# A hybrid decoder trunk on one core: rows of the activations' buffer of 2560 instead of 2112 bytes, low half 1536 instead of 1088 bytes behind the high one, and a dynamic DMA scratch of 8 instead of 16 KB

## Chip, core and metric

The kernel runs on one core of a Trainium2 chip. The metric is the time of one execution in microseconds, as the device measures it; the time of a kernel is the median of its runs. A profile of one execution shows what each engine did: TensorE (PE for matmuls, PEld for the loading of their weights), VectorE (DVE), ScalarE (ACT), GpSimd (POOL), SyncE (SP, which issues DMAs here) and the DMA queues.

## The reference

A sequence of 256 positions of width 1024 passes six sublayers: feed-forward, forgetting attention, feed-forward, then feed-forward, HGRN2 (a gated linear recurrence), feed-forward. Each has an RMS norm with a shift and a scale ahead of it and a gate behind it, which come from a conditioning vector `c`; all in float32. Cut to its core:

```
mod = (silu(c) @ ada_w[i] + ada_b[i]).reshape(B, 3, 3, 1, D)
h = rms_norm(x, norm_g[i, 0]) * (1 + mod[:, 0, 1]) + mod[:, 0, 0]
a, b = split(h @ w_up); x = x + 0.5 * mod[:, 0, 2] * ((silu(a) * b) @ w_down)
h = ...; x = x + mod[:, 1, 2] * (fox_attention(h, ...) or hgrn2(h, ...))
h = ...; x = x + 0.5 * mod[:, 2, 2] * swiglu(h, ...)
return rms_norm(x, final_norm_g)
```

The feed-forward is 1024 to 2 x 2816 and back; the two mixers have four projections of 1024 x 1024 and one back.

## The kernel before

**Split products.** To get float32 results from `float32r` matmuls, every operand is kept as a high and a low half, each 32 bits wide: the high half is the value rounded, the low half what is left. `mm3` (L724 to L731) makes one product of a 128 x 128 piece of weights with the activations of one row: weights' high half times activations' high half (L728), weights' high half times activations' low half (L729), weights' low half times activations' high half (L730), all added into one PSUM tile. Each of the three is 256 columns wide and has its own weight load.

**Where the activations lie.** Two buffers `hbuf[0]` and `hbuf[1]` hold the activations of a sublayer, one for the normed input `h`, the other for the next one (`ubuf`) or for the output of a mixer; `out_proj` swaps them. Each has 8 rows (one for each 128 of the 1024 features; a "row" here is what one partition holds for it). A row has the 256 positions of the high half, then two columns with the norm's shift (`HS`), which the "folded" blocks read along, so that their matmuls of L728 and L730 are 258 columns wide, then a gap, and from column `LO` on the 256 of the low half. `LO` and the row's length `HB` are set at the head of the file:

```
HS = S + 2
LO = S + 16
HB = LO + S
```

The lines that write a low half are L589, L655, L704 and L795, those that read it L729 and L880 (`hl` of L877). The inner activations of the feed-forward lie in another tile, `gx` (in `big`): 22 rows of 512 columns, the low half directly behind the high one, so 1024 bytes behind, with a row every 2048 bytes. Products on `hbuf` write PSUM tiles named `pf`, those on `gx` tiles named `pd`; both go through `mm3`.

**Weights.** SP fetches weights in raw pieces of up to 512 KB into 8 buffers (`raw`), in a fixed order of items (`plan`). ACT copies a piece to `wh` (L369, rounding), DVE subtracts to get `wl` (L370). There are three `wh` and three `wl` buffers of 8 KB per partition; a block of the up projection is 1024 x 256 weights and 48 matmuls. Between the weights stand pieces of the matrices for the conditioning, 512 KB each, which DVE multiplies and adds (L408, L410); their sums pass through PE in `ada_finish` as short matmuls (L469). The order of everything is set by `tick`, which `mm3` calls after each three matmuls: it splits the next piece when it is due and steps the side tasks.

**The start.** The first feed-forward's first 7 blocks run row by row while their weights and the conditioning's matrices arrive (`head_products`, 112 calls of `mm3`).

**Addresses.** All tiles lie one behind the other in each partition, in the order of their making: 16384 bytes of dynamic DMA scratch, four constants of 32 bytes, `big` (45056), `ident` (512), `hbuf[0]`, `hbuf[1]`, the rest. `big`, and with it `gx`, begins at 128 modulo 512; so do `hbuf[0]` (at 62080) and `hbuf[1]` (78976). `wh` and `wl` begin at 448 modulo 512, and each of their rows of 256 columns is 1024 bytes. A row of `hbuf` is 2112 bytes, 4 x 512 + 64, and its low half stands 1088 = 2 x 512 + 64 bytes behind.

| | high half, modulo 512 | low half, modulo 512 |
|---|---|---|
| `gx`, any row | 128 | 128 |
| `hbuf`, row k, before | 128 + 64 k | 192 + 64 k |
| `hbuf`, row k, changed | 128 | 128 |

**Scratch.** It serves the DMAs that POOL issues. There are four: two of a bias (L600), `tm` (L603) and `lmask` (L604).

Of the kernel before, what the change touches and what calls it, by code (L numbers as in the profile page):

```python
# [19 lines left out]
P = 128  # L20
S = 256
# [32 lines left out]
ADA_HEAD = 5  # L54
ADA_TAIL = 6
HS = S + 2
LO = S + 16
HB = LO + S


def shape_constants():
    i = np.arange(P)
    ident = np.eye(P, dtype=np.float32)
    causal = np.where(i[None, :] > i[:, None], np.float32(NEG), np.float32(0)).astype(np.float32)
    lcross = (i[:, None] > i[None, :]).astype(np.float32)
    masks = np.zeros((P, len(LEV), P), np.int32)
    for li, b in enumerate(LEV):
        masks[:, li] = i[:, None] // b == i[None, :] // b
    sel32 = (i[:, None] % 32 == np.arange(32)[None, :]).astype(np.float32)
    selq = np.zeros((P, 16), np.float32)  # L70
    for h in range(16):
        selq[h, h] = -1
        selq[64 + h, h] = -1
    consts = np.concatenate([ident, causal, selq, sel32], axis=1)
    return (np.ascontiguousarray(consts), np.ascontiguousarray(lcross),
            np.ascontiguousarray(masks.reshape(P, -1)))


def flip(x):
    return np.ascontiguousarray(np.concatenate([x[:, :P], x[:, :P - 1:-1]], axis=1))  # L80
# [10 lines left out]
class Trunk:  # L91
# [404 lines left out]
    def setup(self):  # L496
# [82 lines left out]
        for q in range(D // QW):  # L579
# [3 lines left out]
            for k in range(q * n, (q + 1) * n):  # L583
# [4 lines left out]
                v0 = nc.scalar.copy(h[:, :S], u)  # L588
                v1 = nc.vector.tensor_tensor(h[:, LO:LO + S], u, h[:, :S].bitcast(F32), ALU.subtract)  # L589
                self.last_shift = (v0.ins, v1.ins)  # L590
# [58 lines left out]
    def x_ready(self, k):  # L649
        nc = self.nc  # L650
        if self.fold:
            gs = self.mod(*self.fold, "gs")[:, k:k + 1]
            u = self.ubuf[:, k, :]
            nc.scalar.activation(u[:, :S], self.x[:, k, :], AF.Copy, scale=gs)
            nc.vector.scalar_tensor_tensor(u[:, LO:LO + S], self.x[:, k, :], gs, u[:, :S].bitcast(F32),  # L655
                                           ALU.mult, ALU.subtract)
# [43 lines left out]
    def h_shift(self, u, k, l, s, dst):  # L700
        nc = self.nc
        sh = self.mod(l, s, "shift")
        a = nc.scalar.activation(dst[:, k, :S], u, AF.Identity, bias=sh[:, k:k + 1])
        v = nc.vector.scalar_tensor_tensor(dst[:, k, LO:LO + S], u, sh[:, k:k + 1], dst[:, k, :S].bitcast(F32),  # L704
                                           ALU.add, ALU.subtract)
# [162 lines left out]
    def v_token(self, kind, h, dst, func):  # L868
        nc = self.nc
        pss = [self.acc("pv0"), self.acc("pv1")]  # L870
        for kh in range(2):
            wh, wl = self.weights(kind)
            for i in range(4):
                k = kh * 4 + i
                for t in range(2):
                    hh = self.h[:, k, t * P:(t + 1) * P]
                    hl = self.h[:, k, LO + t * P:LO + (t + 1) * P]  # L877
                    nc.tensor.matmul(pss[t], hh, wh[:, i, :], start=(k == 0), stop=False)  # L878
# [392 lines left out]


def build(inputs, subs=(0, 1, 2, 3, 4, 5), final=True):
    nc = bacc.Bacc("TRN2", target_bir_lowering=False, num_devices=1)
    arrays, args = {}, {}
    consts, tmat, lmask = shape_constants()
    every = {n: np.ascontiguousarray(inputs[n]) for n in _INS}
    every["x"] = flip(every["x"])
    every.update(consts=consts, tmat=tmat, lmask=lmask)
    for name, arr in every.items():  # L1280
        arrays[f"in_{name}_dram"] = arr
        args[name] = nc.dram_tensor(f"in_{name}_dram", arr.shape, mybir.dt.from_np(arr.dtype),
                                    kind="ExternalInput").ap()
    out = nc.dram_tensor("out_0_dram", (1, S, D), F32, kind="ExternalOutput").ap()
    with tile.TileContext(nc) as tc:
        with ExitStack() as ctx:
            Trunk(ctx, tc, args, out, list(subs), final).run()
    return nc, arrays
# [6 lines left out]
```

## Time and profile before

| | us |
|---|---|
| median of 3 runs | 1092.43 |
| the three runs | 1087.57, 1092.43, 1092.46 |
| the profiled execution | 1088.01 |
| its span, first to last instruction | 1086.2 |

The mean granted TensorE clock of the profiled execution was 0.994. Its stages, from the rows that write the tiles: the start to about 65 us; the first feed-forward to 216; attention to 365; the second feed-forward to 553; the third to 741; HGRN2 to 888; the last feed-forward and the output to the end. Matmuls are pipelined: the duration that a row of the trace shows for one is longer than the distance to the next one's start.

### The profile page before, as it was taken

The page shows a single profiled execution, that of the slowest core. Times are in us where ns is not written, and L with a number is a line of the kernel's source. Part 1 is how long each engine was busy: PE and PEld are TensorE (multiplying, and loading weights), DVE is VectorE, ACT ScalarE, POOL GpSimd, SP SyncE. Part 2 cuts the span into 40 slices and gives each one's busy share as a digit, 9 for nine tenths or more (in the row PEclk, how much of TensorE's full clock was granted, in tenths as well). Part 3 has the DMA queues.
Part 4 walks back from the last instruction along what each step waited for, and adds up shares of the span by engine and source line. Part 5 has one row for each costly group of instructions (what it writes and reads, how often), then busy time and mean ns, then how long its engine had stood idle before and what let it go on. Part 6 is the DMA issues. An engine that isn't in the chain of part 4 may idle for free.

```text
span 1086.2 us, 22135 instructions
## 1 busy us (share of the span) xinstructions
PE 1058.2 (97%) x8835; PEld 1036.9 (95%) x8835; DVE 882.5 (81%) x1593; ACT 587.0 (54%) x1100; POOL 23.1 (2%) x46
## 2 busy tenths in 40 slices
PE   5999999999999999999999999999999999999997
PEld 5999999988999999999999999999998999999996
DVE  6999999589995999898779999978977879555542
ACT  5464444476864755443555444446677756444443
POOL 0000000020000000000000000000000000000000
PEclk8999999999999999999999999999999999999998
DMA  9999999669784589999959999985633366665531
GB/s 292 337 330 327 330 349 315 176 209 341 251 263 122 156 252 324 331 302 305 263 170 274 335 331 355 318 243 177 211 117 117 118 169 188 187 194 179 179 109 40
DMA packets 304707, 260.26 MB, mean 240 GB/s; under 512 B 9524, under 2 KB 281500, under 8 KB 304604
## 3 DMA queue, kind: packets, MB, share of 16 engines
q1 hardware_dynamic: 304172, 257.80, 77.9%
q8 instruction: 69, 1.13, 0.4%
q0 software_dynamic: 288, 0.52, 0.2%
q10 hardware_dynamic: 144, 0.52, 0.1%
q14 instruction: 34, 0.28, 0.1%
HBM read 257.77 MB, written 1.05 MB: 238 GB/s over the span
## 4 chain that ended last, share of the span: by engine, by line
PE 73%; issue 18%; ACT 3%; DVE 3%; DMA 1%; POOL 1%; SPq 0%; POOLq 0%; DVEq 0%
PE pf L730 16%; PE pf L728 16%; PE pf L729 16%; PE pd L728 6%; PE pd L730 6%; PE pd L729 6%; PE pv L878 1%; PE pv L879 1%; PE pv L880 1%; ACT wh L369 1%; PE sc L999 1%; DVE wl L370 1%; PE pA L1173 1%; DMA raw<-in_ffn_w_up_dram 1%; PE pt L1021 1%
## 5 line engine op out<-in xcount | busy, mean ns | idle before, releaser
L730 PE MATMUL pf<-hbuf,wl 128*128 128x256 f32 (+1 forms) x1920 | 541.7, 283 | 0.0
L729 PE MATMUL pf<-hbuf,wh 128*128 128x256 f32 x1920 | 536.5, 280 | 0.9 <-DVE hbuf L589 0.9
L728 PE MATMUL pf<-hbuf,wh 128*128 128x256 f32 (+1 forms) x1920 | 535.8, 283 | 0.6 <-ACT hbuf L588 0.6
L369 ACT CAST wh<-raw 128x1024 fp32r<-128x1024 f32 x338 | 341.4, 1028 | 284.2 <-PE pf L729 165.4
L370 DVE TENSOR_TENSOR wl<-raw,wh 128x1024 fp32r<-128x1024 f32 x338 | 401.0, 1195 | 107.1 <-ACT wh L369 106.1
L729 PEld LDWEIGHTS pf<-hbuf,wh 128*128 128x128 f32 x1920 | 363.2, 189 | 1.4 <-DVE hbuf L589 1.1
L730 PEld LDWEIGHTS pf<-hbuf,wl 128*128 128x128 f32 x1920 | 361.8, 188 | 0.2 <-issue 0.2
L728 PEld LDWEIGHTS pf<-hbuf,wh 128*128 128x128 f32 x1920 | 359.7, 189 | 1.3 <-ACT hbuf L588 0.7
L728 PE MATMUL pd<-gx,wh 128*128 128x256 f32 x704 | 195.6, 278 | 0.0
L729 PE MATMUL pd<-gx,wh 128*128 128x256 f32 x704 | 194.7, 277 | 0.0
L730 PE MATMUL pd<-gx,wl 128*128 128x256 f32 x704 | 194.7, 277 | 0.0
L410 DVE SCALAR_TENSOR_TENSOR adaacc<-raw,cond,adaacc 128x1024 f32<-128x1024 f32 x112 | 143.7, 1283 | 12.9 <-DMA raw<-in_ada_w_dram 11.7
L728 PEld LDWEIGHTS pd<-gx,wh 128*128 128x128 f32 x704 | 132.4, 188 | 0.1
L729 PEld LDWEIGHTS pd<-gx,wh 128*128 128x128 f32 x704 | 132.2, 188 | 0.0
L730 PEld LDWEIGHTS pd<-gx,wl 128*128 128x128 f32 x704 | 132.2, 188 | 0.0
L793 ACT CAST gx<-g 128x256 fp32r<-128x256 f32 x88 | 35.6, 406 | 66.7 <-DVE g L835 58.2
L795 DVE TENSOR_TENSOR gx<-g,gx 128x256 fp32r<-128x256 f32 x88 | 36.9, 421 | 0.5 <-ACT gx L793 0.2
L835 DVE TENSOR_TENSOR g<-sa,pf 128x256 f32<-128x256 f32 x73 | 30.0, 414 | 0.1
L800 DVE SCALAR_TENSOR_TENSOR x<-pd,mod,x 128x256 f32<-128x256 f32 x32 | 14.3, 479 | 19.0 <-PE pd L730 19.0
L462 DVE STREAM_TRANSPOSE adatr<-adaacc 128x256 f32<-128x256 f32 x64 | 28.4, 443 | 1.5
L463 DVE TENSOR_REDUCE adared<-adatr 128x8 f32<-128x256 f32 x64 | 26.7, 417 | 1.4
L834 ACT ACTIVATE sa<-pf 128x256 f32<-128x256 f32 x73 | 27.4, 376 | 0.0
(219 smaller groups left out, 871.2 us busy)
## 6 DMA issues: line engine op xcount, KB each, us to landing
raw<-in_ffn_w_up_dram SPq DMA_DIRECT2D x162, 512.0 KB, 6.1
raw<-in_ada_w_dram SPq DMA_DIRECT2D x128, 512.0 KB, 6.2
raw<-in_ffn_w_down_dram SPq DMA_DIRECT2D x76, 512.0 KB, 5.5
raw<-in_fox_w_in_dram SPq DMA_DIRECT2D x32, 512.0 KB, 5.2
raw<-in_hgrn_w_in_dram SPq DMA_DIRECT2D x32, 512.0 KB, 4.5
raw<-in_ada_w_dram SPq DMA_DIRECT2D x32, 256.0 KB, 6.7
raw<-in_ffn_w_up_dram SPq DMA_DIRECT2D x16, 448.0 KB, 5.9
raw<-in_fox_w_out_dram SPq DMA_DIRECT2D x8, 512.0 KB, 4.5
```

The source lines that it names most:

```text
L369: nc.scalar.copy(wh[:, ks, cs], raw)
L370: nc.vector.tensor_tensor(wl[:, ks, cs], raw, wh[:, ks, cs].bitcast(F32), ALU.subtract)
L410: nc.vector.scalar_tensor_tensor(self.ada_acc, raw, self.cond[:, k:k + 1], self.ada_acc, ALU.mult, ALU.add)
L462: nc.vector.transpose(tr, total[:, o:o + S])
L463: nc.vector.tensor_reduce(red[:, o // 32:(o + S) // 32], tr.rearrange("p (b j) -> p b j", j=32), AX.X, ALU.add)
L728: nc.tensor.matmul(ps, wh, hx[:, :n], start=first, stop=False, skip_group_check=True)
L729: nc.tensor.matmul(ps[:, :S], wh, hx[:, lo:lo + S], start=False, stop=False, skip_group_check=True)
L730: nc.tensor.matmul(ps, wl, hx[:, :n], start=False, stop=last, skip_group_check=True)
L793: nc.scalar.copy(dst[:, :S], v)
L795: nc.vector.tensor_tensor(dst[:, lo:lo + S], v, dst[:, :S].bitcast(F32), ALU.subtract)
L834: nc.scalar.activation(sa, ps[0], AF.Silu)
L835: nc.vector.tensor_tensor(g, sa, ps[1], ALU.mult)
```

## The change

Two numbers. `LO` is 384 columns instead of 272, so a row of `hbuf` (`HB`) is 640 columns, 2560 bytes, and the low half stands 1536 bytes behind the high one. The unused gap between the shift's columns and the low half grows from 14 to 126 columns. Both buffers grow by 3584 bytes, and the dynamic DMA scratch shrinks from 16384 to 8192 bytes.

```diff
-LO = S + 16
+LO = S + P
 HB = LO + S
...
 def build(inputs, subs=(0, 1, 2, 3, 4, 5), final=True):
-    nc = bacc.Bacc("TRN2", target_bir_lowering=False, num_devices=1)
+    nc = bacc.Bacc("TRN2", target_bir_lowering=False, num_devices=1, dynamic_dma_scratch_size=8192)
```

The instructions of each engine and their order stay as they are; only addresses differ. `big`, `ident` and `hbuf[0]` move down by 8192 bytes, `hbuf[1]` by 4608, all behind it by 1024; every tile begins at the same offset modulo 512 as before.

## Prediction

> **What bounds the kernel now.** I read the page first: busy shares, then the chain that ended last.
>
> ```profile
> span 1086.2 us, 22135 instructions
> ...
> PE 1058.2 (97%) x8835; PEld 1036.9 (95%) x8835; DVE 882.5 (81%) x1593; ACT 587.0 (54%) x1100; POOL 23.1 (2%) x46
> ...
> PE 73%; issue 18%; ACT 3%; DVE 3%; DMA 1%; POOL 1%; SPq 0%; POOLq 0%; DVEq 0%
> PE pf L730 16%; PE pf L728 16%; PE pf L729 16%; PE pd L728 6%; PE pd L730 6%; PE pd L729 6%; PE pv L878 1%; PE pv L879 1%; PE pv L880 1%; ACT wh L369 1%; PE sc L999 1%; DVE wl L370 1%; PE pA L1173 1%; DMA raw<-in_ffn_w_up_dram 1%; PE pt L1021 1%
> ```
>
> TensorE sets the end. The chain lies on the three matmuls of `mm3` (L728 to L730), and 48% of the span on those that write `pf`, which read `hbuf`. The waits say the same: first those of PE, then those of ACT.
>
> ```profile
> PE adac L446 <- DVE adc L434: 3.4, 1, 3.4
> PE pv L546 <- DMA ident<-in_consts_dram: 3.1, 1, 3.1
> ...
> ACT wh L369 <- PE pf L729: 165.4, 70, 7.2
> ...
> ACT wh L358 <- DMA raw<-in_ffn_w_up_dram: 19.8, 9, 3.2
> ```
>
> PE's longest waits are 3.4 and 3.1 us and lie in the start; no weight tile is among them. ACT, which begins each split of a weight, waits 165.4 us for PE to release an old `wh`. So weights stand ready, and what PE needs per matmul is what counts. L358 is the start (the first 65 us), where ACT waits for DMA: nothing is gained there.
>
> **The rate, row by row.** The mean of one matmul (280 ns) is a modelled, pipelined duration; the rate is the distance between starts. First the number of matmuls, from the groups by form:
>
> ```profile
> L729 PE MATMUL pf<-hbuf,wh 128*128 128x256 f32 x1920 | 536.5, 280 | 0.9 <-DVE hbuf L589 0.9
> L730 PE MATMUL pf<-hbuf,wl 128*128 128x256 f32 x1584 | 446.0, 283 | 0.0
> ...
> L730 PE MATMUL pf<-hbuf,wl 128*128 128x258 f32 x336 | 95.7, 285 | 0.0
> ...
> L728 PE MATMUL pd<-gx,wh 128*128 128x256 f32 x704 | 195.6, 278 | 0.0
> ```
>
> So 3 x 1584 = 4752 plain matmuls on `hbuf`, 3 x 336 = 1008 of the folded blocks (two of three with 258 columns), and 3 x 704 = 2112 on `gx`. Now the timeline of PE: first and last row of stretches that hold nothing but `mm3`. On `gx` (187 rows, 186 distances):
>
> ```profile
> 496.79 0.28 PE L729 MATMUL pd<-gx,wh 128*128 128x256 f32 x1
> ...
> 517.87 0.28 PE L729 MATMUL pd<-gx,wh 128*128 128x256 f32 x1
> ```
>
> 21.08 us / 186 = 113.3 ns. On `hbuf`, two stretches (113 rows, then 114 rows):
>
> ```profile
> 465.80 0.28 PE L730 MATMUL pf<-hbuf,wl 128*128 128x256 f32 x1
> ...
> 478.87 0.28 PE L728 MATMUL pf<-hbuf,wh 128*128 128x256 f32 x1
> ...
> 939.77 0.28 PE L729 MATMUL pf<-hbuf,wh 128*128 128x256 f32 x1
> ...
> 953.09 0.28 PE L728 MATMUL pf<-hbuf,wh 128*128 128x256 f32 x1
> ```
>
> 13.07 us / 112 = 116.7 ns and 13.32 us / 113 = 117.9 ns: the same instructions, weights and column count as on `gx`, 3.4 to 4.6 ns slower. They keep one of these two rates until something else passes through PE. Within a stretch the distances depend on the row of `hbuf`:
>
> ```profile
> 943.07 0.29 PE L730 MATMUL pf<-hbuf,wl 128*128 128x256 f32 x1
> 943.20 0.28 PE L728 MATMUL pf<-hbuf,wh 128*128 128x256 f32 x1
> 943.32 0.27 PE L729 MATMUL pf<-hbuf,wh 128*128 128x256 f32 x1
> 943.43 0.28 PE L730 MATMUL pf<-hbuf,wl 128*128 128x256 f32 x1
> ```
>
> Going from row 5 to row 6 they are 0.13, 0.12 and 0.11 us. On `hbuf`, the rows' phase modulo 512 moves by 64 bytes from row to row and the low half stands 64 bytes behind the high one; on `gx` every row and both halves have the same phase, 128. That is what the change gives to `hbuf`. The weights keep their phase (448) in both. The folded blocks (90 rows) and a later stretch on `gx` (88 rows):
>
> ```profile
> 384.75 0.28 PE L728 MATMUL pf<-hbuf,wh 128*128 128x258 f32 x1
> ...
> 395.49 0.28 PE L730 MATMUL pf<-hbuf,wl 128*128 128x258 f32 x1
> ...
> 1049.75 0.28 PE L730 MATMUL pd<-gx,wl 128*128 128x256 f32 x1
> ...
> 1060.00 0.28 PE L730 MATMUL pd<-gx,wl 128*128 128x256 f32 x1
> ```
>
> 10.74 us / 89 = 120.7 ns folded; 10.25 us / 87 = 117.8 ns on `gx`, after four transposes of the output (`fin`) had passed. So equal phases too know a **short state** (113.3) and a **long one** (117.8), and keep either until disturbed.
>
> **The change part by part.** No instruction is added, removed or moved; only addresses differ.
>
> *Plain matmuls.* Of the 4752, 3 x 112 = 336 belong to the start, which waits for DMA. Left: 4416. Their present rate I take as 117.4 ns (a third of the blocks at 116.7, the rest at 117.9; the last feed-forward's row in the table below has 682 in 80 us, two of them across its edges, so 117.6). All in the short state they gain 4.1 ns each, 18.1 us; all in the long one they lose 0.4 ns each, 1.8 us. I take four fifths short: 0.8 x 18.1 - 0.2 x 1.8 = 14.1 us. It is nearer to the short end since on `gx` the long state appears only behind the output's transposes.
>
> *Folded blocks.* Bounds: nothing gained, or 113.3 ns stretched by two columns in two of three (113.9): 6.8 ns x 1008 = 6.9 us. I take their surcharge over the long state (120.7 - 117.8 = 2.9) as kept: 116.2 ns, so 4.5 us, and four fifths of it, 3.6. Sum so far 17.7 us.
>
> *What lies beside.* The same gain has to be fed. Stretches of the span in a table, with DMA share and GB/s last:
>
> ```profile
> 395.00:475.00 80.00, 80.00 (x692) 79.69 (x691) 74.16 (x102) 37.20 (x56) 0.00 (x0) 1.00 1.09 322
> 475.00:525.00 50.00, 50.00 (x448) 49.70 (x447) 46.14 (x64) 22.14 (x32) 0.00 (x0) 1.00 0.89 293
> 600.00:680.00 80.00, 79.99 (x697) 79.46 (x696) 78.00 (x107) 37.07 (x56) 0.00 (x0) 1.00 1.11 340
> ...
> 220.00:365.00 145.00, 141.91 (x1099) 131.30 (x1098) 124.64 (x251) 101.81 (x221) 5.78 (x18) 1.00 0.69 225
> 745.00:880.00 135.00, 131.37 (x1006) 124.71 (x1005) 110.99 (x327) 92.10 (x265) 7.07 (x9) 1.00 0.45 138
> 920.00:1000.00 80.00, 80.00 (x682) 80.00 (x681) 43.26 (x58) 38.41 (x57) 0.00 (x0) 1.00 0.65 190
> ```
>
> The second and third feed-forward (395 to 525, 600 to 680) have DMA full (share over 1) and DVE at 92 to 98%. A 3.5% faster PE wants 333 and 352 GB/s there. In 80 us the shortfall is at most 2.8 us each, and the split weights lying ready (three `wh` buffers, each a block of 48 x 117.9 = 5.7 us) cover most of it; the wait on weights that follows I price at 1.5 us in all, between 0 and the whole gain of the two, 2 x 3.5 = 7 us (816 plain and 240 folded matmuls each). In the attention stages (220 to 365, 745 to 880) PE stands idle for 3.1 and 3.6 us and much of the chain is other work; of their 5 us I take off a third, 1.5 us. The last feed-forward has slack everywhere (DVE 54%, DMA 0.65) and keeps all. So 17.7 - 3 = **14.7 us**.
>
> *Scratch.* It serves the DMAs of POOL alone:
>
> ```profile
> tm<-in_tmat_dram POOLq DMA_DIRECT2D x1, 64.0 KB, 5.8
> ...
> 63.15 0.56 POOL L603 DMA_DIRECT2D tm<-in_tmat_dram  x1 [52.38 <-DVE lmask L602]
> 63.70 0.55 POOL L604 DMA_DIRECT2D lmask<-in_lmask_dram  x1
> 216.23 0.64 POOL L339 MEMSET wh<- 128x640 f32 x1 [151.98 <-PE pd L729]
> ```
>
> The first row is of the DMA view: `tm` lands 5.8 us after its issue. Were the second DMA to wait for that, POOL would be late by 5.8 us, and it has 151.98 us before its next work: cost nothing; with that cover gone, 5.8 us.
>
> *Sum.* The profiled execution took 1088.01 us: 1073.3. The runs shown are 1087.57, 1092.43 and 1092.46, so their median lies 4.4 us above the profiled one, and 1077.7 stands against it. Which of the two levels a median hits I can't tell; I take the middle, **1075 us**.
>
> **The rivals.**
> 1. *Feeding becomes the bound.* DMA at 322 to 340 GB/s can't give more, and the second and third feed-forward win nothing (7 us gone instead of 1.5), the attention stages 1 us less: 1075 + (7 - 1.5) + 1 = 1081.5, and up to 1086 with more of the long state. For it: DVE 98% busy at 600 to 680. Against: ACT waits 165.4 us for PE.
> 2. *Nothing happens.* Either the phase isn't what slows `hbuf`, or the rows settle in the long state everywhere. Then 18.1 us turn into 0 or -1.8 and the folded blocks stay: 1088 to 1093. For it: the 117.8 ns on `gx`. Against: `gx` holds 113.3 for 186 distances on end, at the same weights' phase and column count. The Trainium skill has a rule by which the address can't matter: TensorE: Matmul & The Clock Gate, section Back-to-back issue gap, makes the distance of two matmuls columns / 2.4 + 2.5 ns, with no operand address in it. It would be 109.2 ns on both tiles and the sum 0; the trace disagrees with it in size and in the difference of the tiles.
> 3. *Slower: one phase for all is the bad one.* Weight and activation rows would now collide at every matmul in the same way, instead of at some rows; the folded blocks' 120.7 ns is the slowest steady rate in the trace. At it, 4416 matmuls lose 3.3 ns, 14.6 us: 1105. It decides from 117.4 + 5.5 us / 4416 = 118.6 ns on. Against: `gx` has exactly these phases and runs at 113.3.
> 4. *The change doesn't do what it says,* if `hbuf` no longer began at phase 128. Both row pitches keep the second buffer where the first is, and 7168 bytes more against 8192 less move the rest by 1024: no chance of its own.
>
> **How the numbers follow.** Forecast 62% (1063 to 1080), rival 1 20% (1080 to 1086), rival 2 12% (1087 to 1093; 8 for the long state everywhere, 4 for a phase that plays no part), rival 3 6% (about 1105). Half a percent is about what a measurement of this kernel can tell from no change: 5.5 us, so faster means below 1087. Faster 82%, same 12%, slower 6%. The lower end is all in the short state and nothing lost (18.1 + 6.9 from 1088: 1063); the range 1063 to 1087 leaves out rivals 2 and 3.
>
> **What would show it.** On the timeline, `pf` stretches at 113.3 ns, equal for all rows, would bear out the first step; 117.8 says long state; 116 in the folded blocks the second. If PE gets new waits on `wl` (L370) between 475 and 525 or 690 and 720, rival 1 is at work. `pd` must stay at 113.3, POOL's next work behind its DMAs must stay where it was. The forecast is wrong if `pf` rates stay at 116.7 to 117.9, or if they fall and the span doesn't.

## The result, and the profile after

| | us | runs |
|---|---|---|
| before, median (lowest to highest) | 1089.13 (1087.14 to 1092.46) | 8 |
| changed, median (lowest to highest) | 1084.04 (1079.57 to 1087.62) | 8 |
| changed, the profiled execution | 1083.45, its span 1081.6 | 1 |

The ratio is 0.9946, with a 95% interval of 0.9923 to 0.9968: faster by 5.1 us, 0.54%. The forecast was 1075. Against its own basis, the profiled execution of before, 14.7 us were to go; 4.6 went. The changed kernel's runs spread over 8 us, those of before over 5.

The page of the changed kernel: span, busy shares, and the chain that ended last.

```profile
span 1081.6 us, 22135 instructions
...
PE 1049.0 (97%) x8835; PEld 1027.5 (95%) x8835; DVE 881.6 (82%) x1593; ACT 585.7 (54%) x1100; POOL 23.1 (2%) x46
...
PE 51%; issue 20%; DVE 17%; DMA 7%; ACT 3%; POOL 1%; SPq 0%; POOLq 0%; DVEq 0%; ACTq 0%
PE pf L729 10%; PE pf L728 10%; PE pf L730 10%; DVE wl L370 7%; DMA raw<-in_ada_w_dram 6%; DVE adaacc L410 4%; PE pd L728 4%; PE pd L729 4%; PE pd L730 4%; DVE adatr L462 1%; ACT wh L369 1%; DVE adared L463 1%; PE pA L1173 1%; DVE gx L795 1%; PE sc L999 1%
```

PE is 9.2 us less busy, but the span is only 4.6 us shorter. The chain says why: it ran over PE for 73% of the span and now does for 51%; DVE went from 3 to 17%, DMA from 1 to 7%, and the lines named are the splitting of weights (`wl`) and the conditioning's adds (`adaacc`, raw pieces of `in_ada_w`).

The waits of the changed kernel (total, times, longest), then the first of its kind in the kernel before:

```profile
ACT wh L369 <- PE pf L729: 129.6, 61, 7.2
...
PE adaps L469 <- DVE adared L463: 4.2, 5, 2.4
...
PE pd L730 <- DVE wl L370: 1.8, 2, 1.7
```

```profile
PE adaps L469 <- DVE adared L463: 0.2, 1, 0.2
```

ACT waits less for PE (165.4 before): the stock of split weights is thinner. PE has two new waits, for weights (`wl`) and, larger, for the sums of the conditioning (`adared`).

Where the 4.6 us are, stage by stage (from the first matmul of one stage to that of the next, in both traces). "Forecast" spreads the prediction's own terms by the number of matmuls: 14.1 us / 4416 = 3.2 ns a plain one, 3.6 us / 1008 = 3.6 ns a folded one, 0.75 us taken off in the second and third feed-forward and in each mixer.

| stage | before, us | changed, us | difference | forecast |
|---|---|---|---|---|
| start | 70.2 | 69.3 | -0.9 | 0 |
| first feed-forward, up | 85.3 | 85.6 | +0.3 | -2.3 |
| first feed-forward, down | 60.6 | 62.9 | +2.3 | 0 |
| forgetting attention | 149.5 | 148.7 | -0.8 | -1.7 |
| second feed-forward | 187.6 | 186.2 | -1.4 | -2.7 |
| third feed-forward | 188.6 | 189.8 | +1.2 | -2.7 |
| HGRN2 | 146.2 | 144.6 | -1.6 | -1.8 |
| last feed-forward, output | 198.2 | 194.5 | -3.7 | -3.5 |

The last feed-forward and HGRN2 did what was forecast. The 10.1 us that are missing lie in the first feed-forward (4.9) and in the second and third (5.2); the start and the attention cancel.

**First feed-forward: the long state, and it spills over.** Timeline of the changed kernel, first and last rows of undisturbed stretches: `pf` there (249 rows), `pd` behind it (233), the folded blocks of the second feed-forward (185), and `pf` in the last feed-forward (794 rows).

```profile
70.02 0.28 PE L728 MATMUL pf<-hbuf,wh 128*128 128x256 f32 x1
...
99.23 0.28 PE L730 MATMUL pf<-hbuf,wl 128*128 128x256 f32 x1
...
162.77 0.28 PE L729 MATMUL pd<-gx,wh 128*128 128x256 f32 x1
...
190.09 0.28 PE L730 MATMUL pd<-gx,wl 128*128 128x256 f32 x1
...
374.08 0.28 PE L729 MATMUL pf<-hbuf,wh 128*128 128x256 f32 x1
...
395.95 0.28 PE L730 MATMUL pf<-hbuf,wl 128*128 128x258 f32 x1
...
919.03 0.28 PE L729 MATMUL pf<-hbuf,wh 128*128 128x256 f32 x1
...
1008.91 0.28 PE L730 MATMUL pf<-hbuf,wl 128*128 128x256 f32 x1
```

29.21 us / 248 = 117.8 ns, 27.32 / 232 = 117.8, 21.87 / 184 = 118.9, and 89.88 / 793 = 113.3 ns. So `hbuf` now runs at one of the two rates of equal phases (the prediction's short and long state), and in the whole first feed-forward it is the long one. The same 233 matmuls of the down projection in the kernel before:

```profile
163.12 0.29 PE L729 MATMUL pd<-gx,wh 128*128 128x256 f32 x1
...
189.43 0.28 PE L730 MATMUL pd<-gx,wl 128*128 128x256 f32 x1
```

26.31 us / 232 = 113.4 ns. `gx` was never touched by the change, and lost 4.4 ns: since `hbuf` has its phase now, the state goes on from `pf` to `pd`.

**Second and third feed-forward: PE waits for DVE.** The two largest waits, on the timeline (last column: idle time before the row, and its releaser).

```profile
505.17 0.28 PE L729 MATMUL pd<-gx,wh 128*128 128x256 f32 x1
507.13 0.38 PE L730 MATMUL pd<-gx,wl 128*128 128x256 f32 x1 [1.68 <-DVE wl L370]
...
713.30 0.28 PE L730 MATMUL pd<-gx,wl 128*128 128x256 f32 x1
715.98 0.25 PE L469 MATMUL adaps<-adared,cst 128*32 128x8 f32 x8 [2.41 <-DVE adared L463]
```

The second is a wait that the prediction hadn't thought of: `ada_finish` puts its short matmuls into PE's order a fixed number of ticks (`SUM_LAG`) behind DVE's reductions. When PE is faster and DVE isn't, DVE comes too late and PE, in order, stands still with weights at hand. Six such gaps in the two stages, counted from start to start less a matmul's usual distance each, make 6.5 us; before there was one, of 0.2. DMA has a part in the two largest: DVE's last long idle times ahead of them are waits for a raw piece.

```profile
504.65 1.28 DVE L410 SCALAR_TENSOR_TENSOR adaacc<-raw,cond,adaacc 128x1024 f32<-128x1024 f32 x1 [1.43 <-DMA raw<-in_ada_w_dram]
...
696.92 1.28 DVE L410 SCALAR_TENSOR_TENSOR adaacc<-raw,cond,adaacc 128x1024 f32<-128x1024 f32 x1 [2.98 <-DMA raw<-in_ada_w_dram]
```

The table of stretches, same windows as before (DVE busy is the third pair, DMA share and GB/s last):

```profile
395.00:475.00 80.00, 80.00 (x717) 79.71 (x716) 74.68 (x101) 37.19 (x57) 0.00 (x0) 1.00 1.10 324
475.00:525.00 50.00, 48.16 (x432) 47.47 (x431) 46.06 (x65) 22.04 (x32) 0.00 (x0) 1.00 0.89 291
600.00:680.00 80.00, 78.72 (x700) 78.06 (x699) 77.02 (x106) 36.41 (x57) 0.00 (x0) 1.00 1.09 336
...
920.00:1000.00 80.00, 80.00 (x708) 80.00 (x708) 44.21 (x59) 38.64 (x59) 0.00 (x0) 1.00 0.67 197
```

In the last feed-forward, where DVE has slack, PE starts 708 matmuls instead of 682. At 600 to 680 it stands idle 1.3 us, DMA carries 336 GB/s (340 before), and only 3 matmuls more were done (700 for 697). The waits aren't the only reason there: behind one of them 232 matmuls ran in the long state.

```profile
603.46 0.25 PE L469 MATMUL adaps<-adared,cst 128*32 128x8 f32 x8 [0.62 <-DVE adared L463]
...
603.86 0.28 PE L730 MATMUL pf<-hbuf,wl 128*128 128x256 f32 x1
...
631.07 0.28 PE L730 MATMUL pf<-hbuf,wl 128*128 128x256 f32 x1
```

27.21 us / 231 = 117.8 ns, 1.0 us more than at 113.3.

### The profile page after: what moved, and what is told of

The parts are those of the page before. It is cut to its first block, busy times and chain, and to the rows that moved or that the text cites. A ratio compares the mean times of both kernels' runs of the same rounds, so it can differ in the third digit from the quotient of the medians.

```text
span 1081.6 us, 22135 instructions
## 1 busy us (share of the span) xinstructions
PE 1049.0 (97%) x8835; PEld 1027.5 (95%) x8835; DVE 881.6 (82%) x1593; ACT 585.7 (54%) x1100; POOL 23.1 (2%) x46
## 4 chain that ended last, share of the span: by engine, by line
PE 51%; issue 20%; DVE 17%; DMA 7%; ACT 3%; POOL 1%; SPq 0%; POOLq 0%; DVEq 0%; ACTq 0%
PE pf L729 10%; PE pf L728 10%; PE pf L730 10%; DVE wl L370 7%; DMA raw<-in_ada_w_dram 6%; DVE adaacc L410 4%; PE pd L728 4%; PE pd L729 4%; PE pd L730 4%; DVE adatr L462 1%; ACT wh L369 1%; DVE adared L463 1%; PE pA L1173 1%; DVE gx L795 1%; PE sc L999 1%
## 5 line engine op out<-in xcount | busy, mean ns | idle before, releaser
L730 PE MATMUL pf<-hbuf,wl 128*128 128x256 f32 (+1 forms) x1920 | 534.8, 280 | 0.1
L410 DVE SCALAR_TENSOR_TENSOR adaacc<-raw,cond,adaacc 128x1024 f32<-128x1024 f32 x112 | 143.4, 1281 | 14.1 <-DMA raw<-in_ada_w_dram 13.2
L654 ACT ACTIVATE hbuf<-x,gs 128x256 fp32r<-128x256 f32 x40 | 18.3, 501 | 22.4 <-DVE x L800 22.3
```

The source lines that it names most:

```text
L410: nc.vector.scalar_tensor_tensor(self.ada_acc, raw, self.cond[:, k:k + 1], self.ada_acc, ALU.mult, ALU.add)
L730: nc.tensor.matmul(ps, wl, hx[:, :n], start=False, stop=last, skip_group_check=True)
```

## Experiments

Theory: (1) equal phases of all rows and both halves bring two rates, and which one is entered changes from execution to execution; (2) where PE is faster, DVE and DMA don't feed it. Each experiment also timed the kernel before beside it; ratios are against that.

**1. The changed kernel once more.** No edit.

> The changed kernel once more, to see which rates are fixed and which are luck. Theory (two states, kept until disturbed): stretches on hbuf show 113.3 ns or 117.8 ns per matmul and nothing between; the state of the first feed-forward (117.8 in the profiled execution, down projection too) may differ this time, and the execution's time moves with it by up to about 5 us between 1079 and 1088. Rival (the first feed-forward is always slow, for a reason of its own such as DMA): 117.8 there again, in the down projection too, and a time within 1 us of 1083.5 when the waits for weights are the same.

1084.09 us. The first up projection began at 113.3 ns, turned to 117.8 after a wait of 0.59 us for DVE's sums (`adared`) and stayed there with its down projection; HGRN2's output projection was long (113.3 in the first profile). Directly behind the folded blocks both profiles are short, until the next wait. The waits in the second and third feed-forward recur (four of 0.6 to 2.3 us idle time). So the rates are the same two, and where no folded block leads, what decides between them isn't known. Over the nine profiles of this section in which all rows are equal (`again`, `p256`, `noada_a`, `dvelight`, `dmalight`, `q34_a`, `pool_a`, `tail_a`, and the changed kernel's), the down projection of the first feed-forward was long in four and short in five.

One thing is new. Behind the wait of 2.33 us the granted clock was 0.50 for some 3 us (the clock is the number ahead of the DMA share):

```profile
715.20:718.30 3.10, 3.10 (x16) 3.10 (x17) 3.10 (x7) 1.85 (x5) 0.00 (x0) 0.50 0.96 263
```

Matmuls started 213 ns apart there, which cost another 1.7 us. The same stands behind waits of 1.74 us in `reset7`, 2.62 in `p256`, and 2.08 and 2.21 in `tail_a`, but not behind the changed kernel's 2.41. So a wait can cost more than its idle time.

**2. One equality alone.** `low`: both halves at one phase, which moves by 64 bytes from row to row (rows of 2624 bytes, low half 1536 behind). `pitch`: all rows at one phase, low half 64 bytes off (2560 bytes, 1088 behind). Both have the scratch of 8 KB.

```diff
# low
-LO = S + 16
+LO = S + P
-HB = LO + S
+HB = LO + S + 16
# pitch
 LO = S + 16
-HB = LO + S
+HB = 2 * S + P
# both, in mm3 (and the same for dst in split_act)
-        lo = hx.shape[-1] - S
+        lo = LO if hx.shape[-1] == HB else hx.shape[-1] - S
```

> Half of the change: the low half stands 1536 bytes behind the high one (same phase modulo 512), but a row is 2624 bytes, so the phase still moves by 64 from row to row. Theory (a matmul is slower where the phase of its activations differs from that of the one before): one step in three differs instead of three in three, so the short state is between 113.3 and 116.7, about 114.5 ns. Rival A (only the distance of high and low half counts): 113.3. Rival B (only the rows' pitch counts): 116.7 as before.

> The other half: rows of 2560 bytes, all of one phase, but the low half 1088 bytes behind the high one, so 64 off modulo 512. Theory (a matmul is slower where the phase of its activations differs from that of the one before): two steps in three differ, so the short state is about 115.6 ns. Rival A (only the distance of high and low half counts): 116.7. Rival B (only the rows' pitch counts): 113.3.

1090.34 and 1095.56 us (one run each; before beside them 1087.59 to 1090.18). The rates of both missed all expectations on the slow side; the time of `low`, a single run, can't be told from before. Timeline of `low`, then of `pitch`, 287 rows each in the second up projection:

```profile
428.13 0.28 PE L729 MATMUL pf<-hbuf,wh 128*128 128x256 f32 x1
...
461.97 0.28 PE L730 MATMUL pf<-hbuf,wl 128*128 128x256 f32 x1
```

```profile
429.86 0.28 PE L729 MATMUL pf<-hbuf,wh 128*128 128x256 f32 x1
...
463.97 0.28 PE L730 MATMUL pf<-hbuf,wl 128*128 128x256 f32 x1
```

118.3 and 119.3 ns, against 117.4 before and 113.4 with both. `pitch` also has stretches at 117.8 (245 matmuls from 102.42 us on). The two equalities don't add: each alone costs 1 to 2 ns, both together give 4. In both kernels all `pd` behind `pf` of the first three feed-forwards runs at 113.4: unequal phases in `hbuf` clear the long state before `gx` begins.

**3. The size of the phase, and the scratch.** `p256`: rows of 2304 bytes, low half 1280 behind, equal modulo 256 but not modulo 512. `scratch`: the rows of before with 8 KB.

```diff
# p256
-LO = S + 16
+LO = S + 64
# scratch
-    nc = bacc.Bacc("TRN2", target_bir_lowering=False, num_devices=1)
+    nc = bacc.Bacc("TRN2", target_bir_lowering=False, num_devices=1, dynamic_dma_scratch_size=8192)
```

> Rows of 2304 bytes, low half 1280 behind: rows and halves of one phase modulo 256, not modulo 512. If 256 bytes are enough, the timeline shows the two rates of the changed kernel alone (113.3 and 117.8 ns on hbuf) and the time is 1082 to 1086. If 512 are needed, a mixture of distances by row as before or worse, 116 to 119 ns in the mean, and 1087 to 1096.

> The rows of before with the scratch of 8 KB alone. By every theory here no change: ratio within 0.4% of 1, hbuf at 116.7 and 117.9 ns, gx at 113.3. A rival that the scratch (or where big and the weights lie) did part of it: 1084 to 1087, or slower than 1093.

`p256` took 1083.34 us, ratio 0.9944 (0.9925 to 0.9964), with 113.3 and 117.8 ns on `hbuf`: 256 bytes are enough, with 4 KB per partition less than the change uses. `scratch` took 1089.62, ratio 0.9996 (0.9977 to 1.0015): it costs and gives nothing. The long rows with the old scratch weren't tried.

**4. Breaking the long state.** The eighth row of each buffer moved by 64 bytes, so that in each half block (24 matmuls) one row of eight has another phase. The copy of the shift's columns is split in two for it.

```diff
+class Rows:
...
+    def __getitem__(self, at):
+        p, k, c = at
+        o = k * HB + (16 if k == KC - 1 else 0)
+        return self.t[:, o:o + HB][p, c]
```

> The changed kernel with the eighth row of each buffer moved by 64 bytes. Theory (the long state of equal phases is kept only while phases stay equal; in the kernel before, the down projection began in the short state behind activations of unequal phase each time): no stretch stays at 117.8 ns, each half block of 24 matmuls comes to 113.5 to 114.3 ns on average, the first feed-forward and its down projection included; time about 1079 us, 4 us below the changed kernel. Rival (the step in phase doesn't touch the state): stretches of 117.8 ns as in the changed kernel, and 0.5 ns more everywhere, so about 1086 us.

1083.64 us, ratio 0.9946 (0.993 to 0.9963). Timeline: `pf` in the first up projection (251 rows), `pd` behind it (233).

```profile
70.05 0.28 PE L739 MATMUL pf<-hbuf,wh 128*128 128x256 f32 x1
...
98.58 0.28 PE L740 MATMUL pf<-hbuf,wl 128*128 128x256 f32 x1
...
161.00 0.29 PE L739 MATMUL pd<-gx,wh 128*128 128x256 f32 x1
...
187.31 0.28 PE L740 MATMUL pd<-gx,wl 128*128 128x256 f32 x1
```

114.1 and 113.4 ns: the long state is gone there, as expected. But the time is that of the changed kernel: between the two expectations, with the rates of the theory. The first feed-forward is 4.1 us shorter (144.3 for 148.4 behind the start), the second and third are 3.9 longer. In them `pf` is 0.9 ns slower than in the short state, and the waits of PE grew from 6.5 us to 7.4, with 1.6 us at half the clock behind the last. What one cause gives back, the other takes.

**5. Less to feed.** Of the eight pieces of each streamed conditioning matrix only two are fetched and added, on the changed rows (`noada_a`) and on those of before (`noada_b`).

```diff
-QUOTA = (24, 24, 34, 38)
+QUOTA = (6, 6, 8, 10)
...
-            return [("ada", (l, s, part, k)) for part in parts for k in range(KC)]
+            return [("ada", (l, s, part, k)) for part in parts for k in (0, KC - 1)]
```

> The changed kernel with only the first and the last of the eight pieces of each streamed conditioning matrix fetched and added (three quarters of them left out), so DMA and DVE have slack in every feed-forward. To be read against noada_b, the rows of before with the same pieces left out. Theory 'feeding ate the gain': without new waits of PE the changed rows gain 9 to 13 us over noada_b, and the waits of 0.4 to 2.7 us at the beginnings of the second and third down projection and in the third up projection, 6.3 us in all, are gone. Rival 'feeding plays no part, the rates alone gave what was measured': the gain stays at 4 to 6 us and the waits stay, or go on both sides alike. Third: the states fall otherwise and the up projections are long (117.8 ns) nearly everywhere: gain under 3 us.

> The rows of before (with 8 KB scratch) with only the first and the last of the eight pieces of each streamed conditioning matrix (three quarters left out). PE waits for little there already, so theory and rival agree: 0 to 6 us faster than before, mostly from fewer adds beside the attention; matmuls on hbuf stay at 116.7 to 117.9 ns.

1070.55 (1069.85 to 1073.72) and 1085.08 us (1083.7 to 1085.74): ratios 0.9829 (0.9807 to 0.985) and 0.9951 (0.9936 to 0.9966). The same change of rows now gives 14.5 us instead of 5.1, more than the 9 to 13 expected. In the profile of `noada_a` PE waits for neither `adared` nor `wl` in the second and third feed-forward, and their plain `pf` is at 113.4 ns. From the first folded matmul of the second to the last `pd` of the third, `noada_a`, then `noada_b`:

```profile
360.25 0.28 PE L728 MATMUL pf<-hbuf,wh 128*128 128x258 f32 x1
...
728.77 0.28 PE L730 MATMUL pd<-gx,wl 128*128 128x256 f32 x1
```

```profile
363.92 0.28 PE L728 MATMUL pf<-hbuf,wh 128*128 128x258 f32 x1
...
739.78 0.28 PE L730 MATMUL pd<-gx,wl 128*128 128x256 f32 x1
```

368.5 and 375.9 us, so the rows gain 7.4 us there; with everything fetched and added they gained 0.2 (376.0 before, 375.8 changed). Shown with that: the waits come from the load of feeding that the faster rows meet, not from the rows by themselves. Another part of the 14.5 is luck: the first feed-forward of `noada_a` was short in both projections and gained 2.7 us, where the changed kernel's was long and lost 2.6.

**6. DVE or DMA?** On the changed rows, for pieces 1 to 6 of each matrix: `dvelight` fetches all and adds 32 of 1024 columns; `dmalight` fetches 128 columns and adds at full width.

```diff
# dvelight (the rest of the call, "...", is the same)
+            w = D if k == KC - 1 else 32
-            nc.vector.scalar_tensor_tensor(self.ada_acc, raw, ...)
+            nc.vector.scalar_tensor_tensor(self.ada_acc[:, :w], raw[:, :w], ...)
# dmalight
+                raw = raw[:, None, :P].to_broadcast([P, KC, P])
...
+                w = P if kind == "ada" and 0 < p[3] < KC - 1 else c
+                self.nc.sync.dma_start(v[:, :, :w], srcs[0][1][:, k0:k1, :w])
```

> The changed kernel, all conditioning pieces fetched as before, but of pieces 1 to 6 of each matrix only 32 of 1024 columns are multiplied and added (the rest of those adds left out): DMA as full as before, DVE relieved. If the feeding limit is DVE: about 1070, as with three quarters of the pieces left out, and no new waits of PE at the starts of the second and third down projection. If it is DMA: 1080 to 1084, the waits of 0.4 to 2.7 us stay. If both share it: 1074 to 1080.

> The changed kernel, of conditioning pieces 1 to 6 of each matrix only 128 of 1024 columns fetched (the rest of their transfer left out), and DVE's adds at full width, reading those 128 columns eight times: DVE as loaded as before, DMA relieved by about 40 MB. If the feeding limit is DMA: 1070 to 1074 and no new waits. If it is DVE: 1082 to 1084 with the waits as they were. If both share it: 1075 to 1081.

1073.16 (1072.3 to 1074.36) and 1077.66 us (1073.44 to 1080.53). The third up projection and PE's waits of the whole run, `dvelight` first (window and waits are two views of one kernel, so two fences each):

```profile
584.00:670.00 86.00, 86.00 (x775) 85.56 (x774) 64.12 (x114) 40.92 (x63) 0.00 (x0) 1.00 1.08 331
```

```profile
PE pd L732 <- DVE wl L370: 0.4, 1, 0.4
PE adaps L471 <- DVE adared L465: 0.4, 1, 0.4
```

```profile
584.00:670.00 86.00, 85.74 (x771) 85.23 (x771) 85.14 (x122) 41.77 (x65) 0.00 (x0) 1.00 0.83 238
```

```profile
PE adaps L474 <- DVE adared L468: 1.3, 3, 0.5
PE pd L735 <- DVE wl L371: 1.1, 1, 1.1
```

With DMA as full as ever (331 GB/s) and DVE at 64 of 86 us, the waits are all but gone. With DMA at 238 GB/s and DVE at 85 of 86, 2.4 of 6.0 us of them stay. By the waits DVE is the nearer limit, but the times don't say so. From the first folded matmul of the second feed-forward to the last `pd` of the third the profile of `dvelight` takes 372.4 us (678 of its matmuls were long) and that of `dmalight` 370.8 (83 long), against 375.8 in the changed kernel and 368.5 in `noada_a`. Of the 6.2 us between these two executions (1080.53 and 1074.36) 4.5 are the state in the first feed-forward, most of it long in `dmalight` and short in `dvelight` (147.8 and 143.3 us). So DVE and DMA share the limit, and relieving either brings back much of the gain; which is the nearer isn't shown. That `dvelight` is 12 us below `noada_b`, where still less is fetched and added (ratios to before 0.9837 and 0.9951), shows that the gain of the rows itself returns, not only that of the adds left out.

**7. Moving the load to the attention, nothing left out.** 10 pieces from the second and third feed-forward to the attention, on the changed rows and on those of before.

```diff
-QUOTA = (24, 24, 34, 38)
+QUOTA = (24, 34, 30, 32)
```

> The changed kernel with 10 of the conditioning's pieces moved from the second and third feed-forward (34 to 30 and 38 to 32) to the forgetting attention (24 to 34), where the DMA share is 0.58 to 0.80. Theory 'feeding ate the gain': 10 pieces are 5.2 MB, about 16 us of DMA at 330 GB/s, so the 6.3 us of waits in the two feed-forwards shrink to under 2 and the kernel is 3 to 5 us faster than the changed one (about 1079), unless DVE in the attention (about 73 of 80 us busy at 220 to 300) gives 1 to 3 back. Rival 'no feeding': 1084, waits as before.

> The rows of before (8 KB scratch) with the same 10 pieces moved. By both theories nothing to gain, since PE waited for no weights there: 1087 to 1091; 1 to 3 us slower if DVE in the attention becomes late.

1090.46 and 1099.24 us. Both expectations missed: the attention can't take it. In the profiles PE waits there for `wl` and `adared` on both rows, 0.2 to 2.5 us each, 6.5 us in all on the changed rows and 6.8 on the others, where it had been 0.5 and 0.2; behind the longest the clock fell to 0.50 again (1.7 and 1.5 us more). The changed rows still gain 8.8 us over the others.

**8. Moving a third of the adds to GpSimd, nothing left out.** On the changed rows (`pool_a`), on those of before (`pool_b`), and on the rows of experiment 4 (`pool_r`).

```diff
+        eng = nc.gpsimd if part == 2 and l + s else nc.vector
...
+            eng.tensor_scalar(raw, raw, self.cond[:, k:k + 1], None, ALU.mult)
+            eng.tensor_tensor(self.ada_acc, raw, self.ada_acc, ALU.add)
```

> The changed kernel; the third matrix of each streamed sublayer (40 of 120 pieces) is multiplied and added by GpSimd instead of VectorE, nothing left out. Theory 'VectorE's load feeds too slowly': VectorE is relieved by some 13 of 80 us in a feed-forward, the waits of PE in the second and third fall below 2 us in all, and the time is 1075 to 1080. Rival 'DMA is the limit': 1082 to 1085. Second rival 'GpSimd and VectorE slow each other' (adds or splits get longer than 1.2 us each): 1084 to 1100.

> The rows of before (8 KB scratch) with the same adds on GpSimd. VectorE isn't waited for there: 1086 to 1091 by the theory and by the DMA rival; 1091 to 1105 if GpSimd and VectorE slow each other. The difference to pool_a is the gain of the rows: 8 to 13 us by the theory, 4 to 6 if feeding is not relieved.

> pool_a with the eighth row of each buffer moved by 64 bytes, which breaks the long state at every half block. If long state and feeding are the two causes and nothing else: first feed-forward at about 114.4 and its down projection at 113.4 ns in the profile, waits below 2 us: 1074 to 1078. If feeding isn't relieved: 1082 to 1085, as without GpSimd.

1187.35, 1191.96 and 1186.24 us. GpSimd's groups in `pool_a` (count, busy, mean ns, idle before):

```profile
L413 POOL TENSOR_SCALAR raw<-raw,cond 128x1024 f32<-128x1024 f32 x35 | 110.5, 3158 | 268.6 <-DMA raw<-in_ada_w_dram 268.6
L414 POOL TENSOR_TENSOR adaacc<-raw,adaacc 128x1024 f32<-128x1024 f32 x35 | 88.3, 2522 | 2.6
```

A piece takes 5.7 us there, against 1.28 on DVE. PE waits 37.8 us in all for sums (`adared`), and 19.4 us at one place for `wl`; that eight pieces in a row hold their raw buffers and keep weights out is likely, and not shown. The experiment says nothing on its question.

**9. Spreading the load to the end of the down projection, nothing left out.** On the changed rows (`tail_a`), on those of before (`tail_b`), on the rows of experiment 4 (`tail_r`).

```diff
-            span = max(nm - ADA_TAIL - head, 1)
+            span = max(nm - (ADA_TAIL if pos < 2 else 0) - head, 1)
```

> The changed kernel; in the second and third feed-forward the conditioning's pieces are spread over 30 instead of 24 items of weights, to the end of the down projection, where VectorE is 81% busy (58 of 72 us) instead of 93 to 97%. Nothing is left out. Per item there are 1.13 and 1.27 pieces instead of 1.42 and 1.58, so a stretch of 80 us in the up projection has 4 pieces less, 5 us of VectorE. Theory 'VectorE and DMA feed too slowly': the waits of PE there fall from 6.3 us to under 2.5, the time is 1078 to 1081.5. Rival 'the waits are not from the mean load, but from single bursts such as the transposes of the conditioning': 1083 to 1085, waits as before, at other places. Second rival: the later pieces delay the next sublayer's norm: 1086 to 1090, with waits of PE at 553 or 742 us.

> The rows of before (8 KB scratch) with the same spread. PE waits for little there: 1087 to 1090.5 by theory and first rival; slower by 2 to 5 us by the second. The gain of the rows, tail_a against tail_b, is 7 to 11 us by the theory and 4 to 6 by the first rival.

> tail_a with the eighth row moved by 64 bytes, which breaks the long state at every half block, at 0.9 ns a matmul elsewhere. Theory: first feed-forward near 114.4 ns, waits under 3 us, 1077 to 1081. If feeding isn't relieved: 1083 to 1085, like the eighth row alone.

1084.82 (1079.81 to 1091.77), 1094.04 (1089.26 to 1096.97) and 1085.09 us (1082.17 to 1086.12). The changed rows are 9.2 us faster than those of before, as the theory had it, but since the others lost 4 us, not since these gained. The profiled execution of `tail_a` (1091.28, near the top of its runs): the window that was worst, then waits.

```profile
584.00:670.00 86.00, 86.00 (x770) 85.71 (x769) 75.77 (x105) 39.07 (x60) 0.00 (x0) 1.00 1.04 309
```

```profile
PE pd L730 <- DVE wl L370: 8.7, 6, 2.2
...
PE adaps L469 <- DVE adared L463: 0.5, 1, 0.5
```

The third up projection has no idle time of PE any more and DVE 10 us of slack: there the theory held. The waits moved into the down projections, for weights now, and grew; in this profile the clock of 0.50 behind them cost another 4.2 us. The time, and waits at other places, are what the first rival said; whether its bursts make them stays open. In the third down projection DVE is 60 of 71 us busy and DMA has a share of 0.86, so the mean load alone doesn't explain it; raw buffers held by late pieces may, which wasn't tried.

No version that leaves nothing out was faster than the changed kernel beyond the interval; `p256`, the eighth row and `tail_r` are equal to it.

## Why the prediction was right in kind and wrong in size

Two steps of the sum failed. The price of feeding, 1.5 us, was 6.3 us of new waits; and the long state, which was given a fifth of the plain matmuls on `hbuf` and none of those on `gx`, took the whole first feed-forward, where 2.3 us were to be won and 2.6 were lost.

- **The mechanism** (equal phases bring `hbuf` to the rates of `gx`): right. 113.3 ns over 794 matmuls on end in the last feed-forward, where nothing else limits PE. That its 3.7 us come so near to the forecast's 3.5 is partly luck: all 816 plain matmuls were short and gained 4.5 ns instead of 3.2 each, the folded ones 1.6 instead of 3.6.
- **"All in the short state" for four fifths of the plain matmuls**: the share of the long state was too small, and its place wrong. It took the whole first feed-forward (720 matmuls at 117.8 instead of 113.3, a forecast gain of 2.3 us turned into +0.3) and 232 matmuls of the third. About 31% of the plain matmuls on `hbuf` behind the start were long in this profile, 36% in `again`. In part this is bad luck, as experiment 1 shows for the first feed-forward. The reason given, that "the long state appears only behind the output's transposes", came from the kernel before, where unequal rows of `hbuf` cleared the state ahead of every `gx`. The change removes what clears it. Nor are the transposes the only way in: on the rows of before a wait of 2.71 us for `wl` left 392 matmuls on `gx` at 117.8 ns (`q34_b`, from 523.85 us on).
- **"`pd` must stay at 113.3"**: wrong, by the same step. 528 matmuls at 117.8: +2.3 us that no term of the sum held. Experiments 2 and 4 show it from the other side: with any unequal row in `hbuf`, the `pd` of the first feed-forward is at 113.4 again.
- **Folded blocks**, 3.6 us: mis-sized. They went from 120.5 to 118.9 ns, 1.6 ns each, 1.6 us in all. 118.9 is what the profiles with equal rows show in them, whichever state the blocks ahead were in; the 116.2 that the prediction made of a short rate and a surcharge was not seen.
- **Feeding**, 1.5 us between 0 and 7: mis-sized. Against 6.9 us to be won in the two feed-forwards by the forecast's rates, 6.3 us of new waits came. The bound held, the value taken was the wrong end of it. It leaned on ACT's 165.4 us of waits for PE, a sum over the whole span; 64 us of them lie in these two stages, but they speak of `wh` alone, and what PE came to wait for is DVE's work. DVE's 78 of 80 us at 600 to 680, with DMA at a share of 1.11, was the row to go by. (DMA wasn't full everywhere: at 475 to 525, where the longest wait for `wl` came, the table has a share of 0.89 and not over 1.) The stretch's means hid the other half: PE waits not for weights alone but for DVE's sums too, and no stock of weights covers that. Rival 1 had this place right and, with 1081.5 to 1086, the time; but it named DMA, where DVE has at least as large a part, and half of what was missing lay in the first feed-forward, which it had only as "more of the long state".
- **Attention and HGRN2**: 2.4 us came of 3.5 forecast.
- **Scratch at nothing**: right, 0.9996 by itself. On the timeline of the changed kernel POOL's work behind its DMAs stands at 217.90 (216.23 before), still behind 154.53 us of waiting for PE.

```profile
62.26 0.56 POOL L603 DMA_DIRECT2D tm<-in_tmat_dram  x1 [52.11 <-DVE lmask L602]
...
217.90 0.64 POOL L339 MEMSET wh<- 128x640 f32 x1 [154.53 <-PE pd L729]
```

- **The level**: the medians of before lay at 1088.6 to 1090.7 in the experiments; the 1.7 us that were added to the sum for it (1075 for 1073.3) were a small matter.

Both missing parts together are 10.1 us of 10.1, and with feeding relieved the rows gave 14.5, what the sum had said with its feeding at 1.5. That sum is not borne out term by term by it: in that profile the first feed-forward was short, and the folded blocks stayed at 118.9 ns.

Still open: what enters the long state (waits of PE, the start and the output's transposes stand in front of it, but not each time); when a wait is followed by a clock of 0.50; which of DVE and DMA is the nearer limit; why one equality alone is worse than none; what limits the down projections in experiment 9; and whether a later place of the conditioning's matmuls in PE's order (a larger `SUM_LAG`) would win back the larger part of the waits, which wasn't tried.

## What to carry to other kernels

When one engine gets faster in every stage, price each stage apart: look there for the engine that is nearly full already (here DVE at 92 to 98%, with DMA beside it), and for every instruction on the faster engine that waits for it at a fixed place in the order, not only for its main feed. A sum of waits over the whole span says nothing on the worst stage, and one helper that waits (ACT) says nothing on another (DVE). And a rate that keeps a state belongs to the neighbours too: making two streams alike can carry a bad state from one into the other.

## What was not expected of the hardware

- A matmul's rate depends on how the offsets of successive moving operands compare: at 256 float32r columns 113.3 or 117.8 ns where rows and halves agree modulo 256, 116.7 or 117.8 in the rows of before, 118.3 where only the halves agree, 119.3 or 117.8 where only the rows agree. The Trainium skill's rule (TensorE: Matmul & The Clock Gate, section Back-to-back issue gap) knows no such term; none of these is 109.2 ns, an estimate from its formula for a single isolated gap.
- The state outlives a change of tile, weights and PSUM target (`pf` to `pd`) and the conditioning's short matmuls in between; one 64-byte step among 8 rows is enough to leave it, at 0.9 ns a matmul.
- Behind some waits of PE of 1.7 to 2.6 us the granted clock fell to 0.50 for 3 to 4 us (213 ns a matmul), which cost about 1.6 us more.
- GpSimd took 3.16 us for a scaling and 2.52 us for an add of 128 x 1024 float32 numbers (means of 35 in `pool_a`), where DVE does both in one instruction of 1.28 us.
